# The FFN norm of a hybrid diffusion block: table load moved ahead, dg products of a tile queued together, the second tile's residual moved ahead

## The chip, the cores and the metric

One core of one Trainium2 chip. The metric is the device time of one execution in microseconds (us), as the median of several runs. PE is the matrix engine, ACT the scalar engine, DVE the vector engine, SP the queue that issues the loads.

## The reference

The kernel computes one layer of a parallel-branch backbone block for 256 tokens of width 2048, all in fp32. The change lies where the mixer's half ends and the feed-forward half (FFN) begins:

```
        x = x + g_m * yl
        x = x + g_f * _swiglu(_rmsnorm(x, norm_ffn_w[l]) * (1 + sc_f) + sh_f,
                              w_ffn_gate[l], w_ffn_up[l], w_ffn_down[l])
```

Here `yl = merged @ w_out` is the mixer's output, `_rmsnorm` divides each token's row by the root of its mean square, and `_swiglu(h)` is `(silu(h @ w_gate) * (h @ w_up)) @ w_down`, with `w_gate` and `w_up` of 2048x5632. The layer ends with a last RMSNorm.

## The kernel before

**Products in three terms.** Every large product is made in a rounded format, so each fp32 operand is split into a high part and a low part. `split` (L123 to L125) does it with a CAST on ACT (the high part, L124) and a subtraction on DVE (the low part, L125). `mm3` (L130 to L133) then issues three products: high by high (L131), activation high by weight low (L132), activation low by weight high (L133). One 128-row piece of the contraction for one half of the tokens is thus three products of 128x512.

**Stages.** The whole kernel is one list of stages. A stage is 256 rows of one weight matrix, 512 columns wide: it is loaded into one of 5 `raw` buffers, split into one of 3 `whi`/`wlo` pairs (or into a longer-lived `hhi`/`hlo` pair where `held=True`), and then multiplied. `stream` walks the list. Before the products of stage i it issues the loads up to stage i+5 and the splits up to stage i+2 (`LEAD` is 2), so the CAST and subtraction of a later stage's weights stand in the queues of ACT and DVE ahead of the work that stage i itself issues there. The order of instructions on each engine is the order in which this code is written, and each engine runs its own queue strictly in order. With 3 pairs, the CAST of one stage waits until PE is done with the stage three before it.

**Two token tiles.** The 256 tokens are two tiles of 128, tile 0 and tile 1, and the 2048 channels are four blocks of 512, numbered n. For the last block of `w_out` (`phase_o(3)`) the eight stages (p from 0 to 7, 256 rows each) are arranged so that tile 0 ends first: for p up to 4 both tiles are multiplied (`mm_both`), for the last three (`APART` is 3) first tile 0 alone (`mm_first`), and then tile 1 for these three together (`mm_second`). The first three stages of the gate matrix (`APART2` is 3) go the same way: `mm_gate0(p)` multiplies tile 0 for p = 0, 1, 2, then `mm_gate1` multiplies tile 1 for the three; `mm_gate(p)` from p = 3 on does both. Gate stages 0 and 1 need block 0 of the normalised activations, stages 2 and 3 block 1, stages 4 and 5 block 2.

**The norm of one tile**, with these names:
- `residual(n, t, ps)` (L1160 to L1165): DVE multiplies the accumulator `ps` by the gate `gm` and adds the input rows `xr`, giving `x`; ACT squares it and sums the row into `xss`.
- `rstd` (L1153 to L1158): DVE sums the four blocks' sums (`r`, L1155), ACT takes the root (L1156), DVE the reciprocal (L1157).
- `preload_sqrt` (L1149 to L1151): an ACT instruction on one column, ahead of which the compiler puts the load of the table set with the root.
- `dg` (L1173): DVE scales the identity matrix by `r`, so that a product of `x` with `dg` (L1182) both turns the tile so that channels lie on partitions and divides each row by its norm. A block has four such fp32 products, and the trace counts each as two passes of PE. They go into one of the four `aux` accumulators.
- `h`: the four pieces of a block are scaled by `Af` and shifted by `Sf`: on ACT for even blocks (L1188), on DVE for odd ones (L1186).
- `h2h`, `h2l`: the high and low part of `h` (L124 and L125), which the gate products take.

Of the kernel before, what the change touches and what calls it, by code (L numbers as in the profile page):

```python
# [11 lines left out]
F32 = mybir.dt.float32  # L12
F32R = mybir.dt.float32r
AF = mybir.ActivationFunctionType
ALU = mybir.AluOpType

P = 128
# [52 lines left out]
APART, APART2 = 3, 3  # L70
# [12 lines left out]
def hybrid_block(ctx: ExitStack, tc, io):  # L83
# [3 lines left out]
    V, S, T = nc.vector, nc.scalar, nc.tensor  # L87
# [12 lines left out]
    def nm(s):  # L100
        names[0] += 1
        return f"{s}{names[0]}"
# [4 lines left out]
    def H(shape, dt=F32, nme="h"):  # L107
        return hp.tile(shape, dt, tag="H", name=nm(nme))

    def Q(shape, dt=F32, nme="q"):  # L110
        return qp.tile(shape, dt, tag="Q", name=nm(nme))

    def acc(shape=(P, CH)):
        return psp.tile(list(shape), F32, tag="acc", name=nm("acc"))

    def aux(shape=(P, CH)):
        return psp.tile(list(shape), F32, tag="aux", name=nm("aux"))

    def C(shape, dt=F32, nme="c"):
        n = nm(nme)  # L120
        return cst.tile(shape, dt, tag=n, name=n)

    def split(hi, lo, src):  # L123
        S.copy(hi, src)  # L124
        V.tensor_tensor(lo, src, hi.bitcast(F32), ALU.subtract)  # L125
# [4 lines left out]
    def mm3(out, ah, al, bh, bl, first, last):  # L130
        T.matmul(out, ah, bh, start=first, stop=False)  # L131
        T.matmul(out, ah, bl, start=False, stop=False)  # L132
        T.matmul(out, al, bh, start=False, stop=last)  # L133
# [34 lines left out]
    def spawn(key, gen, front=False):  # L168
        beside.insert(0, (key, gen)) if front else beside.append((key, gen))
# [9 lines left out]
    def need(*keys):  # L179

        for key in keys:
            while key not in ended:
                credit[0] -= abs(step(next(e for e in beside if e[0] == key)))
# [32 lines left out]
    def add(src, n, mm, **kw):  # L216
        stages.append(Stage(src, n, mm, **kw))
        return stages[-1]
# [7 lines left out]
    ONE, ID = cc[:, CC_ONE : CC_ONE + P], cc[:, CC_ID : CC_ID + P]  # L226
# [210 lines left out]
    Af = C([P, KT], nme="Af")  # L437
    Sf = C([P, KT], nme="Sf")
# [4 lines left out]
    class Ada:  # L443
# [4 lines left out]
        def __init__(self, off, h, kt):  # L448
            self.off, self.h, self.kt = off, h, kt
            c0 = off + h * 1024  # L450
            self.src = w_ada[kt * P : (kt + 1) * P, c0 : c0 + 1024]
# [56 lines left out]
    def ada_keys(*offs):  # L508
        return [f"ada{off}{h}" for off in offs for h in range(2)]
# [328 lines left out]
    def mm_pair(ps, op, p, parts, ts, first, last):  # L838
        hi, lo = parts
        for t in ts:  # L840
            for k in range(2):
                ah, al = op(2 * p + k, t)
                mm3(ps[t], ah, al, hi[:, k, :], lo[:, k, :], first and k == 0, last and k == 1)
# [299 lines left out]
    x1 = [None] * 4  # L1143
    xss = C([P, 2, 4], nme="xss")
    h2h = [None] * 4
    h2l = [None] * 4
    xrs = {}

    def preload_sqrt(dep):  # L1149
        j = C([P, 1], nme="pre")  # L1150
        S.activation(j, dep, AF.Sqrt)  # L1151

    def rstd(ss, n):  # L1153
        r = C([P, n], nme="r")
        V.tensor_reduce(r, ss, mybir.AxisListType.X, ALU.add)  # L1155
        S.activation(r, r, AF.Sqrt, bias=eps, scale=1.0 / D)  # L1156
        V.reciprocal(r, r)  # L1157
        return r  # L1158

    def residual(n, t, ps):  # L1160
        xo = x1[n]
        V.tensor_tensor(xo[:, t, :], ps, gm[n][:, n % 2, :], ALU.mult)
        V.tensor_tensor(xo[:, t, :], xo[:, t, :], xrs[n][:, t, :], ALU.add)
        junk = Q([P, CH], nme="junk")
        S.activation(junk, xo[:, t, :], AF.Square, accum_out=xss[:, t, n : n + 1])  # L1165

    def norm_ffn(t):

        if t == 0:
            preload_sqrt(xss[:, 0, 0:1])  # L1170
        r = rstd(xss[:, t, :], 1)
        dg = Q([P, P], nme="dg")
        V.tensor_scalar(dg, ID, r, None, ALU.mult)  # L1173
        if t == 0:
            for n in range(4):
                h2h[n], h2l[n] = H([P, 4, 256], F32R, nme="h2h"), H([P, 4, 256], F32R, nme="h2l")

        def turn(n):
            ps = aux([P, 4, P])
            hf = Q([P, 4, P], nme="h2")  # L1180
            for c in range(4):
                T.matmul(ps[:, c, :], x1[n][:, t, c * P : (c + 1) * P], dg, start=True, stop=True)  # L1182
            for c in range(4):
                kt = 4 * n + c
                if n % 2:
                    V.tensor_scalar(hf[:, c, :], ps[:, c, :], Af[:, kt : kt + 1], Sf[:, kt : kt + 1], ALU.mult, ALU.add)  # L1186
                else:
                    S.activation(hf[:, c, :], ps[:, c, :], AF.Identity, bias=Sf[:, kt : kt + 1], scale=Af[:, kt : kt + 1])  # L1188
            o = slice(t * P, (t + 1) * P)
            split(h2h[n][:, :, o], h2l[n][:, :, o], hf)  # L1190

        return turn

    op_m, op_h2 = pair_op(mh, ml), pair_op(h2h, h2l)
    pg0 = []
# [1 line left out]
    def ask_x(n):  # L1197
        xrs[n] = H([P, 2, CH], nme="xr")
        load(xrs[n], x[:, n * CH : (n + 1) * CH].rearrange("(t p) n -> p t n", p=P))
        x1[n] = H([P, 2, CH], nme="x1")  # L1200

    def phase_o(n):
        def first():
            need("M0", "M1", "M2")
            ask_x(n)

        def run(ps):
            need(*ada_keys(G_M)[n // 2 : n // 2 + 1])
            for t in range(2):
                residual(n, t, ps[t])  # L1210
                yield 1.2

        if n < 3:
            tokens(io["w_out"], 0, KT, n * CH, op_m, lambda ps: spawn(f"o{n}", run(ps), True), first)
            if n == 0:
                stages[-2].first = lambda: need("M3")
            return

        ps = []
        turns = {}  # L1220
        n_o = 8 - APART
        held = []

        def mm_both(p):
            def mm(parts):
                if p == 0:
                    ps.extend((acc(), acc()))
                mm_pair(ps, op_m, p, parts, range(2), p == 0, False)
            return mm

        def mm_first(p):
            def mm(parts):
                held.append(parts)
                mm_pair(ps, op_m, p, parts, (0,), False, p == 7)
                if p == 7:
                    need("o0", "o1", "o2", *ada_keys(G_M, SC_F, SH_F))
                    residual(3, 0, ps[0])
                    turns[0] = norm_ffn(0)
            return mm

        def mm_second(parts):
            for p in range(n_o, 8):
                mm_pair(ps, op_m, p, held[p - n_o], (1,), False, p == 7)
            turns[0](0)
            residual(3, 1, ps[1])
            turns[1] = norm_ffn(1)
            for i in range(1, 4):
                turns[0](i)

        held2 = []  # L1250

        def mm_gate0(p):
            def mm(parts):
                if p == 0:
                    pg0.extend((acc(), acc()))
                held2.append(parts)
                mm_pair(pg0, op_h2, p, parts, (0,), p == 0, False)
                if p == APART2 - 1:
                    turns[1](0)
            return mm  # L1260

        def mm_gate1(parts):
            for p in range(APART2):
                if p + 1 < 4:
                    turns[1](p + 1)
                mm_pair(pg0, op_h2, p, held2[p], (1,), p == 0, False)
            for i in range(APART2 + 1, 4):
                turns[1](i)

        def mm_gate(p):  # L1270
            def mm(parts):
                mm_pair(pg0, op_h2, p, parts, range(2), False, p == 7)
            return mm

        for p in range(n_o):
            add(rows(io["w_out"], 2 * p, 2, 3 * CH, CH), CH, mm_both(p), first=(lambda: ask_x(3)) if p == 0 else None)
        for p in range(n_o, 8):
            add(rows(io["w_out"], 2 * p, 2, 3 * CH, CH), CH, mm_first(p), held=True, room=0)
            stages[-1].lead = p - n_o + 3
        add(None, 0, mm_second, room=0)  # L1280
        for p in range(APART2):
            add(rows(io["w_ffn_gate"], 2 * p, 2, 0, CH), CH, mm_gate0(p), room=0, held=p == 0)
        add(None, 0, mm_gate1, room=0)
        for p in range(APART2, 8):
            st = add(rows(io["w_ffn_gate"], 2 * p, 2, 0, CH), CH, mm_gate(p))
        st.after.append(lambda: (tanh_gate(0, pg0), spawn("a0", silu(0, pg0), True)))
# [292 lines left out]
```

## Time and profile before

| | |
|---|---|
| median of 3 runs | 1893.85 us (1893.33 to 1894.34) |
| the profiled execution, its own time | 1891.34 us |
| its span in the trace | 1889.5 us |
| PE busy | 1837.7 us, 97% of the span |
| DVE busy, ACT busy | 1249.3 us (66%), 851.5 us (45%) |
| mean granted clock of PE | 0.994 |

The span runs from the first to the last instruction that the profiler records; the execution's own time has 1.84 us around it. All stretches are read from the profiled execution, whose time is 2.51 us below the median of the three runs. A row of the timeline gives the start in us from the span's start, the duration, the engine, the line, the operation, out<-in, the count, and in brackets how long the engine was idle before it and who ended that. Products overlap on PE: one of 128x512 lasts 0.39 us and the next starts 0.227 us after it.

### The profile page before, as it was taken

The numbers are of one execution on the slowest core, as the hardware profiler recorded it, in microseconds if no ns is written. First come the engines' busy times: TensorE is split into PE (matmuls) and PEld (weight loads), VectorE is DVE, ScalarE is ACT, GpSimd is POOL, SyncE is SP. The second block draws the span as 40 slices with busy tenths as digits, with TensorE's granted clock in tenths as the row PEclk, the third lists the DMA queues.
The fourth block names the chain that finished last, engine by engine and source line by source line (L and its number), as shares of the span: only waits on it lengthen the run. The fifth ranks groups of instructions, "written<-read, shape, count | busy, mean of one in ns | idle before, by whom it ended". The sixth has DMA issues, their size and how long they took to land.

```text
span 1889.5 us, 23230 instructions
## 1 busy us (share of the span) xinstructions
PE 1837.7 (97%) x8796; PEld 1482.7 (78%) x8796; DVE 1249.3 (66%) x1524; ACT 851.5 (45%) x1200; POOL 0.2 (0%) x4
## 2 busy tenths in 40 slices
PE   5999999999999999999999998999999999999997
PEld 3667887777777777878788777888888888888886
DVE  4435784878787578887777755777655555555567
ACT  4323445647446464544444444444443444434444
POOL 0000000000000000000000000000000000000000
PEclk9999999999999999999999998999999999999999
DMA  9992342567667557888888854888756666656654
GB/s 325 355 349 76 112 123 67 168 183 228 196 211 224 150 162 232 292 267 304 284 292 292 294 182 134 281 267 303 262 189 191 195 184 190 193 195 189 191 190 143
DMA packets 211904, 409.19 MB, mean 217 GB/s; under 512 B 14672, under 2 KB 47568, under 8 KB 211792
## 3 DMA queue, kind: packets, MB, share of 16 engines
q1 hardware_dynamic: 211792, 407.71, 67.2%
q8 instruction: 69, 1.13, 0.2%
q14 instruction: 43, 0.35, 0.0%
HBM read 405.56 MB, written 2.10 MB: 216 GB/s over the span
## 4 chain that ended last, share of the span: by engine, by line
PE 90%; DVE 4%; ACT 3%; DMA 1%; issue 1%; SPq 1%; DVEq 0%; ACTq 0%
PE acc L131 26%; PE acc L132 26%; PE acc L133 26%; PE aux L314 2%; ACT whi L124 1%; PE aux L131 1%; DVE wlo L125 1%; PE aux L133 1%; PE aux L132 1%; PE aux L683 1%; PE aux L759 1%; SPq L105 1%; PE aux L1317 1%; PE aux L777 1%; DMA raw<-w_ada 0%
## 5 line engine op out<-in xcount | busy, mean ns | idle before, releaser
L125 DVE TENSOR_TENSOR wlo<-raw,whi 128x1024 fp32r<-128x1024 f32 x548 | 668.8, 1223 | 546.9 <-ACT whi L124 543.8
L124 ACT CAST whi<-raw 128x1024 fp32r<-128x1024 f32 x548 | 574.2, 1052 | 758.2 <-PE acc L133 650.6
L131 PE MATMUL acc<-whi,h2h 128*128 128x512 f32 x700 | 274.2, 392 | 5.9 <-ACT h2h L124 5.9
L133 PE MATMUL acc<-whi,h2l 128*128 128x512 f32 x700 | 273.2, 390 | 0.0
L132 PE MATMUL acc<-wlo,h2h 128*128 128x512 f32 x700 | 273.1, 390 | 0.0
L131 PE MATMUL acc<-whi,lh 128*128 128x512 f32 x640 | 256.6, 401 | 0.0
L132 PE MATMUL acc<-wlo,lh 128*128 128x512 f32 x640 | 249.6, 390 | 0.2 <-DVE wlo L125 0.2
L133 PE MATMUL acc<-whi,ll 128*128 128x512 f32 x640 | 249.6, 390 | 0.0
L131 PEld LDWEIGHTS acc<-whi,h2h 128*128 128x128 f32 x700 | 131.8, 188 | 33.6 <-ACT h2h L124 6.5
L133 PEld LDWEIGHTS acc<-whi,h2l 128*128 128x128 f32 x700 | 131.8, 188 | 28.4 <-DVE h2l L125 0.9
L461 DVE SCALAR_TENSOR_TENSOR adacc<-araw,sil,adacc 128x1024 f32<-128x1024 f32 x120 | 153.4, 1278 | 0.0
L132 PEld LDWEIGHTS acc<-wlo,h2h 128*128 128x128 f32 x700 | 131.9, 188 | 27.1
L132 PEld LDWEIGHTS acc<-wlo,lh 128*128 128x128 f32 x640 | 120.3, 188 | 26.9 <-issue 2.2
L131 PEld LDWEIGHTS acc<-whi,lh 128*128 128x128 f32 x640 | 120.2, 188 | 26.4 <-issue 1.5
L133 PEld LDWEIGHTS acc<-whi,ll 128*128 128x128 f32 x640 | 120.1, 188 | 25.5
L131 PE MATMUL acc<-whi,ah 128*128 128x512 f32 x336 | 131.0, 390 | 0.0
L133 PE MATMUL acc<-whi,al 128*128 128x512 f32 x336 | 130.7, 389 | 0.0
L132 PE MATMUL acc<-wlo,ah 128*128 128x512 f32 x336 | 130.7, 389 | 0.0
L131 PE MATMUL acc<-hh,whi 128*128 128x512 f32 x256 | 104.9, 410 | 3.6 <-ACT whi L124 3.6
L132 PE MATMUL acc<-hl,whi 128*128 128x512 f32 x256 | 100.7, 393 | 0.0
L133 PE MATMUL acc<-hh,wlo 128*128 128x512 f32 x256 | 100.5, 392 | 0.0
L133 PEld LDWEIGHTS acc<-whi,al 128*128 128x128 f32 x336 | 63.1, 188 | 13.1
(292 smaller groups left out, 2265.5 us busy)
## 6 DMA issues: line engine op xcount, KB each, us to landing
raw<-w_in SPq DMA_DIRECT2D x208, 512.0 KB, 4.2
araw<-w_ada SPq DMA_DIRECT2D x128, 512.0 KB, 4.9
raw<-w_ffn_gate SPq DMA_DIRECT2D x88, 512.0 KB, 4.5
raw<-w_ffn_up SPq DMA_DIRECT2D x88, 512.0 KB, 3.8
raw<-w_ffn_down SPq DMA_DIRECT2D x88, 512.0 KB, 3.6
raw<-w_ada SPq DMA_DIRECT2D x64, 512.0 KB, 9.4
raw<-w_ssd_out SPq DMA_DIRECT2D x32, 512.0 KB, 5.4
raw<-w_out SPq DMA_DIRECT2D x32, 512.0 KB, 5.0
```

Source lines behind the costliest of these rows:

```text
L105: nc.sync.dma_start(dst, src)
L124: S.copy(hi, src)
L125: V.tensor_tensor(lo, src, hi.bitcast(F32), ALU.subtract)
L131: T.matmul(out, ah, bh, start=first, stop=False)
L132: T.matmul(out, ah, bl, start=False, stop=False)
L133: T.matmul(out, al, bh, start=False, stop=last)
L314: T.matmul(aps[j][32 * k : 32 * k + 32, o], stat[:, 4 * p + k, :], raws[j, i][:, k, :], start=p == 0, stop=p == 3)
L461: V.scalar_tensor_tensor(a, self.raw, sil[:, kt : kt + 1], a, ALU.mult, ALU.add)
L683: T.matmul(ps, btk[:, 2 + t, :], xc[d][t], start=t == 0, stop=t == 1)
L759: T.matmul(seg, m, rh, start=n == 0, stop=n == 3)
L777: T.matmul(yps[b][(h % 2) * 64 : (h % 2) * 64 + 64, i // 2, t * P : (t + 1) * P], xl[:, t, h * HD : (h + 1) * HD], W[:, i, :], start=True, ...
L1317: T.transpose(ps[:, k, t * P : (t + 1) * P], a[t][:, c * P : (c + 1) * P], ID)
```

## The change

1. `preload_sqrt` is no longer called in the norm of tile 0 but in `mm_first` of the first of the three last stages of `w_out`. Its table load and its small instruction stand three stages earlier in ACT's queue.
2. `norm_ffn` and its closure `turn` are replaced by a class `Turn`, which issues the parts of a tile's norm singly: `norm` (root and `dg`), `mm(n)` (the four products of a block with `dg`), `mod(n)` (scale and shift to `h`), `cast(n)` (`h2h`), `low(n)` (`h2l`).
3. For tile 0, the products of all four blocks are written ahead of any `h`. The residual of tile 1 (its DVE part `residual_add`) follows the `h` of block 0, ahead of the `h` of block 1 and of every subtraction `h2l`; its squares follow the CAST of block 0.
4. The rest of tile 0 (blocks 2 and 3) is written behind the products of gate stage 0.
5. For tile 1, blocks 0 and 1 are written together, products, `h`, CAST and subtraction, behind gate stage 2 of tile 0; blocks 2 and 3 together behind gate stage 1 of tile 1. Before, block 0 stood there alone, and one block each stood ahead of a gate stage of tile 1.

The number of instructions of each kind is the same before and after.

```diff
-        if t == 0:
-            preload_sqrt(xss[:, 0, 0:1])
...
         def mm_first(p):
             def mm(parts):
+                if p == n_o:
+                    preload_sqrt(xss[:, 0, 0:1])
                 held.append(parts)
                 mm_pair(ps, op_m, p, parts, (0,), False, p == 7)
                 if p == 7:
                     need("o0", "o1", "o2", *ada_keys(G_M, SC_F, SH_F))
                     residual(3, 0, ps[0])
-                    turns[0] = norm_ffn(0)
+                    turn[0].norm()
...
         def mm_second(parts):
+            a, b = turn
             for p in range(n_o, 8):
                 mm_pair(ps, op_m, p, held[p - n_o], (1,), False, p == 7)
-            turns[0](0)
-            residual(3, 1, ps[1])
-            turns[1] = norm_ffn(1)
-            for i in range(1, 4):
-                turns[0](i)
+            for n in range(4):
+                a.mm(n)
+            a.mod(0)
+            residual_add(3, 1, ps[1])
+            a.mod(1)
+            a.cast(0)
+            residual_sq(3, 1)
+            a.low(0)
+            b.norm()
+            a.cast(1)
+            a.low(1)
...
                 mm_pair(pg0, op_h2, p, parts, (0,), p == 0, False)
+                if p == 0:
+                    for n in (2, 3):
+                        a.mod(n)
+                    for n in (2, 3):
+                        a.cast(n)
+                        a.low(n)
                 if p == APART2 - 1:
-                    turns[1](0)
+                    for n in range(2):
+                        b.mm(n)
+                        b.mod(n)
+                    for n in range(2):
+                        b.cast(n)
+                        b.low(n)
...
         def mm_gate1(parts):
+            b = turn[1]
             for p in range(APART2):
-                if p + 1 < 4:
-                    turns[1](p + 1)
                 mm_pair(pg0, op_h2, p, held2[p], (1,), p == 0, False)
-            for i in range(APART2 + 1, 4):
-                turns[1](i)
+                if p == 1:
+                    for n in (2, 3):
+                        b.mm(n)
+                        b.mod(n)
+                    for n in (2, 3):
+                        b.cast(n)
+                        b.low(n)
```

In the built programs the order shows as follows (out<-in; the numbers tell buffers apart and differ between the two programs). First ACT's queue at the end of `w_out`, before (-) against after (+); `hhi` and `whi` are the high parts of weights, `junk` the squares of `x`:

```order
 L124 CAST hhi_9152<-raw_9096 128x1024
-L124 CAST hhi_9164<-raw_9130 128x1024
-L124 CAST whi_9168<-raw_9148 128x1024
-L124 CAST whi_9182<-raw_9150 128x1024
-L1165 ACTIVATE junk_9194,xss_391<-x_9055 128x512
 L1151 ACT_TABLE_LOAD
-L1151 ACTIVATE pre_9196<-xss_391 128x1
+L1151 ACTIVATE pre_9156<-xss_391 128x1
+L124 CAST hhi_9166<-raw_9130 128x1024
+L124 CAST whi_9170<-raw_9148 128x1024
+L124 CAST whi_9184<-raw_9150 128x1024
+L1167 ACTIVATE junk_9196,xss_391<-x_9055 128x512
```

The table load has moved ahead of three CASTs of gate weights (stages 0, 1, 2) and ahead of the squares of tile 0's last block.

Next DVE's queue from tile 0's `dg` (the first row) on, before:

```order
L1173 TENSOR_SCALAR dg_9202<-cc_73,r_9198 128x128
L125 TENSOR_TENSOR h2l_9205<-h_9231,h2h_9204 128x4x128
L1162 TENSOR_TENSOR x_9055<-acc_9057,g_6359 128x512
L1163 TENSOR_TENSOR x_9055<-x_9055,xr_9053 128x512
L1155 TENSOR_REDUCE r_9246<-xss_391 128x1
L1157 RECIPROCAL r_9246<-r_9246 128x1
L1173 TENSOR_SCALAR dg_9250<-cc_73,r_9246 128x128
L1186 TENSOR_SCALAR h_9253<-aux_9252,Af_382,Sf_383 128x128 x4
L125 TENSOR_TENSOR h2l_9207<-h_9253,h2h_9206 128x4x128
```

and after:

```order
L1182 TENSOR_SCALAR dg_9202<-cc_73,r_9198 128x128
L1162 TENSOR_TENSOR x_9055<-acc_9057,g_6359 128x512
L1163 TENSOR_TENSOR x_9055<-x_9055,xr_9053 128x512
L1195 TENSOR_SCALAR h_9249<-aux_9227,Af_382,Sf_383 128x128 x4
L1207 TENSOR_TENSOR h2l_9255<-h_9242,h2h_9254 128x4x128
L1155 TENSOR_REDUCE r_9260<-xss_391 128x1
L1157 RECIPROCAL r_9260<-r_9260 128x1
L1182 TENSOR_SCALAR dg_9264<-cc_73,r_9260 128x128
L1207 TENSOR_TENSOR h2l_9267<-h_9249,h2h_9266 128x4x128
```

The residual of tile 1 (L1162, L1163) now stands ahead of the first `h2l`, and the `h` of block 1 (four instructions) ahead of the second tile's root and `dg` (from L1155 on), behind which it stood.

Last ACT's queue in the norm of tile 1, from the CAST of gate stage 3's weights (the first row) on, before:

```order
L124 CAST whi_9304<-raw_9162 128x1024
L1188 ACTIVATE h_9315<-aux_9314,Sf_383,Af_382 128x128 x4
L124 CAST h2h_9204<-h_9315 128x4x128
L124 CAST whi_9328<-raw_9178 128x1024
L124 CAST h2h_9206<-h_9333 128x4x128
L1188 ACTIVATE h_9351<-aux_9350,Sf_383,Af_382 128x128 x4
L124 CAST h2h_9208<-h_9351 128x4x128
L124 CAST h2h_9210<-h_9369 128x4x128
```

and after:

```order
L124 CAST whi_9304<-raw_9164 128x1024
L1197 ACTIVATE h_9319<-aux_9314,Sf_383,Af_382 128x128 x4
L1203 CAST h2h_9254<-h_9319 128x4x128
L1203 CAST h2h_9266<-h_9329 128x4x128
L124 CAST whi_9340<-raw_9180 128x1024
L1197 ACTIVATE h_9361<-aux_9356,Sf_383,Af_382 128x128 x4
L1203 CAST h2h_9288<-h_9361 128x4x128
L1203 CAST h2h_9292<-h_9371 128x4x128
```

The `h2h` of block 1 now stands ahead of the CAST of gate stage 4's weights (`whi_9328` before, `whi_9340` after), behind which it stood. On PE the order is the same but for one group: the four products with `dg` of tile 1's block 2 have moved from ahead of gate stage 1 of tile 1 to behind it.

More of the change, by code (lines that the diff above doesn't have):

```diff
@@ L1158, in rstd, with residual_add @@
         return r
-    def residual(n, t, ps):
+    def residual_add(n, t, ps):
         xo = x1[n]
@@ L1163, in residual, with residual_sq @@
         V.tensor_tensor(xo[:, t, :], xo[:, t, :], xrs[n][:, t, :], ALU.add)
+    def residual_sq(n, t):
         junk = Q([P, CH], nme="junk")
-        S.activation(junk, xo[:, t, :], AF.Square, accum_out=xss[:, t, n : n + 1])
-    def norm_ffn(t):
-        if t == 0:
-            preload_sqrt(xss[:, 0, 0:1])
[L1171 to L1180, printed above, removed]
+        S.activation(junk, x1[n][:, t, :], AF.Square, accum_out=xss[:, t, n : n + 1])
@@ L1181, in turn, with residual, __init__, norm @@
+    def residual(n, t, ps):
+        residual_add(n, t, ps)
+        residual_sq(n, t)
+    class Turn:
+        def __init__(self, t):
+            self.t, self.ps, self.hf = t, {}, {}
+        def norm(self):
+            r = rstd(xss[:, self.t, :], 1)
+            self.dg = Q([P, P], nme="dg")
+            V.tensor_scalar(self.dg, ID, r, None, ALU.mult)
+        def mm(self, n):
+            self.ps[n] = aux([P, 4, P])
             for c in range(4):
-                T.matmul(ps[:, c, :], x1[n][:, t, c * P : (c + 1) * P], dg, start=True, stop=True)
+                T.matmul(self.ps[n][:, c, :], x1[n][:, self.t, c * P : (c + 1) * P], self.dg, start=True, stop=True)
+        def mod(self, n):
+            self.hf[n] = Q([P, 4, P], nme="h2")
@@ L1183, in turn @@
             for c in range(4):
                 kt = 4 * n + c
+                a, b = Af[:, kt : kt + 1], Sf[:, kt : kt + 1]
                 if n % 2:
-                    V.tensor_scalar(hf[:, c, :], ps[:, c, :], Af[:, kt : kt + 1], Sf[:, kt : kt + 1], ALU.mult, ALU.add)
+                    V.tensor_scalar(self.hf[n][:, c, :], self.ps[n][:, c, :], a, b, ALU.mult, ALU.add)
                 else:
-                    S.activation(hf[:, c, :], ps[:, c, :], AF.Identity, bias=Sf[:, kt : kt + 1], scale=Af[:, kt : kt + 1])
@@ L1189, in turn, with cast, low @@
-            o = slice(t * P, (t + 1) * P)
-            split(h2h[n][:, :, o], h2l[n][:, :, o], hf)
-        return turn
+                    S.activation(self.hf[n][:, c, :], self.ps[n][:, c, :], AF.Identity, bias=b, scale=a)
+        def cast(self, n):
+            if h2h[n] is None:
+                h2h[n], h2l[n] = H([P, 4, 256], F32R, nme="h2h"), H([P, 4, 256], F32R, nme="h2l")
+            o = slice(self.t * P, (self.t + 1) * P)
+            S.copy(h2h[n][:, :, o], self.hf[n])
+        def low(self, n):
+            o = slice(self.t * P, (self.t + 1) * P)
+            V.tensor_tensor(h2l[n][:, :, o], self.hf[n], h2h[n][:, :, o].bitcast(F32), ALU.subtract)
@@ L1219, in phase_o @@
         ps = []
-        turns = {}
+        turn = (Turn(0), Turn(1))
         n_o = 8 - APART
@@ L1253, in mm @@
             def mm(parts):
+                a, b = turn
                 if p == 0:
```

## The prediction

> **What bounds the kernel now.** I read the first part of the page, then windows around the norm, then the timelines of PE, ACT and DVE there. The page says that PE is the bound:
>
> ```profile
> PE 1837.7 (97%) x8796; PEld 1482.7 (78%) x8796; DVE 1249.3 (66%) x1524; ACT 851.5 (45%) x1200; POOL 0.2 (0%) x4
> ```
>
> Windows of 3.4 us, which is how long the stretches at half clock in PE's rows last (columns: stretch, length, busy time and count of PE, PEld, DVE, ACT, POOL, granted clock, DMA share, GB/s):
>
> ```profile
> 1121.50:1124.90 3.40, 1.81 (x12) 1.30 (x11) 0.61 (x3) 2.03 (x5) 0.00 (x0) 1.00 0.57 219
> 1131.70:1135.10 3.40, 1.73 (x6) 1.16 (x7) 1.66 (x5) 2.37 (x6) 0.00 (x0) 1.00 0.00 0
> 1135.10:1138.50 3.40, 3.40 (x17) 3.30 (x15) 2.41 (x6) 1.36 (x3) 0.00 (x0) 0.51 0.00 0
> 1148.70:1152.10 3.40, 0.90 (x3) 0.48 (x4) 2.48 (x6) 1.57 (x5) 0.00 (x0) 1.00 0.51 141
> 1152.10:1155.50 3.40, 3.40 (x9) 2.66 (x10) 1.97 (x5) 1.33 (x4) 0.00 (x0) 0.52 0.06 18
> 1157.30:1400.00 242.70, 242.70 (x1092) 201.26 (x1091) 168.78 (x162) 104.87 (x112) 0.00 (x0) 1.00 0.79 262
> ```
>
> From 1157.30 on PE has no gap for 242 us. In the norm it has gaps, and after a window with 1.73 or 0.90 us of work in 3.40 the clock falls to half for the next 3.4 us (0.51, 0.52); after one with 1.81 it stays at 1.00. PE's timeline, the rows at each gap:
>
> ```profile
> 1122.25 0.39 PE L133 MATMUL acc<-hhi,ftl 128*128 128x512 f32 x1
> 1124.23 3.81 PE L1182 MATMUL aux<-dg,x 128*128 128x128 f32 x32 [1.59 <-DVE dg L1173]
> 1127.79 0.48 PE L131 MATMUL acc<-hhi,h2h 128*128 128x512 f32 x1
> 1128.34 0.49 PE L133 MATMUL acc<-hhi,h2l 128*128 128x512 f32 x1
> 1130.53 0.40 PE L133 MATMUL acc<-whi,h2l 128*128 128x512 f32 x1
> 1133.37 0.50 PE L131 MATMUL acc<-whi,h2h 128*128 128x512 f32 x1 [2.45 <-ACT h2h L124]
> 1135.13 3.58 PE L1182 MATMUL aux<-dg,x 128*128 128x128 f32 x16
> 1141.08 0.50 PE L131 MATMUL acc<-hhi,h2h 128*128 128x512 f32 x1 [2.37 <-ACT h2h L124]
> 1151.20 0.50 PE L131 MATMUL acc<-whi,h2h 128*128 128x512 f32 x1 [3.43 <-ACT h2h L124]
> 1157.28 0.39 PE L131 MATMUL acc<-whi,h2h 128*128 128x512 f32 x1
> ```
>
> The last row is the first product of gate stage 4. From 1122.48 (1122.25 and the 0.23 that a product takes before the next) to there it is 34.8 us. The work is 64 passes with `dg` at 0.111 (32 in 1124.23 to 1127.79) and 48 products at 0.227, together 18.0 us. So about 16.8 us are gaps and half clock; that is the most that any order can save here.
>
> **The first gap: the table load.** ACT's timeline:
>
> ```profile
> 1110.24 3.89 ACT L124 CAST hhi<-raw 128x1024 fp32r<-128x1024 f32 x4
> 1115.35 1.05 ACT L124 CAST whi<-raw 128x1024 fp32r<-128x1024 f32 x1 [1.22 <-DMA raw<-w_ffn_gate]
> 1117.47 1.05 ACT L124 CAST whi<-raw 128x1024 fp32r<-128x1024 f32 x1 [1.07 <-DMA raw<-w_ffn_gate]
> 1121.88 1.28 ACT L1151 ACT_TABLE_LOAD   x1
> 1125.39 1.50 ACT L1188 ACTIVATE h<-aux,Sf,Af 128x128 f32<-128x128 f32 x4 [1.83 <-PE aux L1182]
> 1126.93 0.62 ACT L124 CAST h2h<-h 128x512 fp32r<-128x512 f32 x1
> 1129.63 0.63 ACT L1165 ACTIVATE junk<-x 128x512 f32<-128x512 f32 x1 [2.08 <-DVE x L1163]
> 1130.58 0.29 ACT L1156 ACTIVATE r<-r,eps 128x1 f32<-128x1 f32 x1 [0.22 <-DVE r L1155]
> 1137.41 0.62 ACT L124 CAST h2h<-h 128x512 fp32r<-128x512 f32 x1 [2.04 <-DVE h L1186]
> 1146.91 1.04 ACT L124 CAST whi<-raw 128x1024 fp32r<-128x1024 f32 x1 [5.88 <-PE acc L133]
> 1150.53 0.62 ACT L124 CAST h2h<-h 128x512 fp32r<-128x512 f32 x1 [2.57 <-DVE h L1186]
> 1166.71 1.28 ACT L1296 ACT_TABLE_LOAD   x1
> ```
>
> and DVE's:
>
> ```profile
> 1118.55 1.23 DVE L125 TENSOR_TENSOR wlo<-raw,whi 128x1024 fp32r<-128x1024 f32 x1 [0.90 <-ACT whi L124]
> 1119.70 0.68 DVE L1162 TENSOR_TENSOR x<-acc,g 128x512 f32<-128x512 f32 x1
> 1121.89 0.16 DVE L1155 TENSOR_REDUCE r<-xss 128x1 f32<-128x4 f32 x1 [0.79 <-ACT junk L1165]
> 1123.79 0.29 DVE L1173 TENSOR_SCALAR dg<-cc,r 128x128 f32<-128x128 f32 x1
> 1127.58 0.69 DVE L125 TENSOR_TENSOR h2l<-h,h2h 128x512 fp32r<-128x512 f32 x1 [3.50 <-ACT h2h L124]
> 1128.90 0.69 DVE L1163 TENSOR_TENSOR x<-x,xr 128x512 f32<-128x512 f32 x1
> 1130.39 0.16 DVE L1155 TENSOR_REDUCE r<-xss 128x1 f32<-128x4 f32 x1 [0.79 <-ACT junk L1165]
> 1130.91 0.16 DVE L1157 RECIPROCAL r<-r 128x1 f32<-128x1 f32 x1 [0.36 <-ACT r L1156]
> 1131.11 0.28 DVE L1173 TENSOR_SCALAR dg<-cc,r 128x128 f32<-128x128 f32 x1
> 1131.31 1.36 DVE L1186 TENSOR_SCALAR h<-aux,Af,Sf 128x128 f32<-128x128 f32 x4
> ```
>
> In tile 0 `dg` starts 1.90 us after the row sum (1121.89 to 1123.79), in tile 1, where no load is in between, 0.72 (1130.39 to 1131.11). Without it `dg` starts at 1122.61 and PE, 0.44 later as before, at 1123.05: 1.18 earlier.
>
> What the load costs at its new place: the third CAST of the row at 1110.24 ends about 1113.2, so the load, and about 0.11 of its small instruction, push the fourth to 1114.6 and the next from 1115.35 to 1115.6; the one at 1117.47 waits for its transfer, so the delay ends there with 0.8 us to spare. The subtraction at 1118.55 and the residual behind it stay. Cost 0; the buffers freed some tenths later are loaded for stages that run 20 us later.
>
> [...] The row at 1166.71 stands right behind a CAST and takes 1.28, with no drain to be seen; I take that.
>
> **Tile 0, blocks 0 and 1.** PE's order does not change. Passes at 1123.05 to 1126.61; `h` of block 0 on ACT 1.16 behind PE's start (as 1124.23 to 1125.39), its CAST at 1125.75 to 1126.37. DVE does the residual of tile 1 meanwhile: 1.4 us from 1122.8, since PE ended tile 1's products at 1122.64. It is hidden under the wait of 3.50 that stood at 1127.58. Then `h` of block 1, when two blocks' passes are out: 1125.10 to 1126.46. Only then `h2l` of block 0, so the third gate product is at 1127.25, 0.6 behind the first instead of 0.55. From there to the 12th product's end as before (1128.34 to 1130.53, and 0.23): 1129.67.
>
> Tile 1's squares follow the CAST at 1126.3 (before 1129.63), the row sum at 1127.11, `dg` 0.72 later at 1127.83. The CAST of block 1 goes behind the root, at 1127.6 to 1128.2, its `h2l` to 1128.93. Both are ready before PE asks at 1129.67, so the gap of 2.45 is gone: gate stage 2 starts 3.70 earlier (1129.67 against 1133.37), and with no wait for its `h2l` its six products end at 1131.03, against 1135.13.
>
> **Tile 1.** `dg` has waited since 1128. Blocks 0 and 1 take 16 passes at full clock, 1.78, to 1132.81 (before 3.58 at half clock). ACT meanwhile ends blocks 2 and 3 of tile 0 (1.5 + 0.6 + 0.6, to 1130.9; CAST at 1137.41 before) and the CAST of gate stage 3 (to 1131.8), DVE likewise to 1133.1. So `h` of block 0 runs at 1132.19 to 1133.69, `h2h` at 1133.73 to 1134.35, the first product at 1134.40 and, behind `h` of block 1 and `h2l`, the third at 1135.21. This gap of 1.6 stays; it was 2.37 behind a half-clock stretch, with the product at 1141.08. So 6.68 earlier.
>
> The CAST at 1146.91 is where most of the rest goes. It waits 5.88 for PE, because its buffer is that of gate stage 1, whose tile 1 products come late; block 1's `h` and `h2h` (1150.53) stand behind it, and PE waits 3.43 for them. After, block 1 stands ahead of it: `h2h` ends at 1135.1, `h2l` at 1135.8. PE runs 12 products to 1137.48, 16 passes of blocks 2 and 3 to 1139.26, six products to 1140.62 and the 12 of gate stage 3 to 1143.34, where it was 1157.28.
>
> What is late next: blocks 2 and 3 of tile 1 now start only behind those 12 products. CAST of gate stage 4 at 1137.7, `h` at 1138.7, `h2h` at 1140.9, `h2l` of block 2 at about 1142.0; PE asks for it in tile 1 of gate stage 4 at 1143.34 + 1.36 = 1144.7. It is hidden with 2.7 us to spare. No DMA is moved; the loads of the next weights start earlier, when DVE frees their buffers.
>
> **The sum**: 1.18 (table) + 2.52 (second gap) + 0.40 (stage 2) + 2.58 (tile 1's first block) + 7.26 (the last gap, with its half clock) = 13.9 us off the span. The profiled execution would take 1891.34 - 13.9 = 1877.4; the median lies 2.51 above that execution, so the median should be about 1880.
>
> Unknown: the clock. A gap of 1.6 with the short wait at the third product leaves 1.7 to 1.9 us of work if it falls into one window, between the rows of 1.73 and 1.81 that decided differently; half clock for 3.4 us costs 1.7. I take none, since the windows may also split the gap, and keep 0 to 3.4 (two windows) for the range. The three half-clock windows of before may be two or four in another execution: 1.7 to either side.
>
> [...]
>
> **Rivals.**
> - Tile 1's first block stays the wait it was. If `h2h` came 5.95 behind the start of the passes, as before (1135.13 to 1141.08), the first product would be at 1136.98, 2.6 later than I have it, and a half-clock window would follow: 13.9 - 2.6 - 1.7 = 9.6, so 1884. For it: ACT is the chain there in both. Against: what held ACT (CAST at 1137.41, then the one behind it) is done by 1131.8.
> - The gain is given back downstream: DMA runs at a share of 0.79 in 1157.30 to 1400, and a PE that comes 14 us earlier could catch the loads. Against: loads are paced by buffers that PE itself frees, so all moves together, and PE has no gap there. If all is given back, 1894, no change.
> - Slower: blocks 2 and 3 of tile 1 come too late for gate stage 4. They have 2.7 us; past that each us is lost, and the kernel becomes slower only when they come 2.7 + 13.9 = 16.6 us later, by over 0.2% at 20.4. Their chain of a CAST, four `h`, two more CASTs and a subtraction is 5 us long, so only an order that lets them wait for a whole further stage could do it. At 21 us late the time would be 1898.
>
> **Chances.** My forecast 0.82, the first rival 0.09, given back 0.06, slower 0.03. The predicted time is 1880. The range goes down by 1.7 (one more half-clock window before) and some for step errors to 1877, and up past the first rival and its own window to 1886. Two runs of this kernel differ by about 0.05%; I call within 0.2% (1890.1 to 1897.6) no change. Faster 0.91, same 0.06, slower 0.03.
>
> **What would show it.** Right: no ACT_TABLE_LOAD between the squares and the root of tile 0; first `dg` pass some 0.4 us behind the last product; no gap at gate stage 2 of tile 0; one gap of 1 to 2 us at gate stage 0 of tile 1, and none behind it; about 20.9 us from 1122.5 to the first product of gate stage 4. Wrong: a CAST of weights that still stands waiting for PE ahead of an `h2h` that PE wants, a gap ahead of gate stage 4, or half-clock windows after the 1.6 us gap.

## The result, and the profile after

| | before | after |
|---|---|---|
| median | 1893.59 us (6 runs, 1892.11 to 1894.88) | 1879.74 us (6 runs, 1877.50 to 1880.89) |
| span of the profiled execution | 1889.5 us | 1876.9 us |
| last w_out product to gate stage 4, on PE | 34.80 us | 20.62 us |

The ratio is 0.9926 (95% interval 0.9915 to 0.9937): 0.74% faster. The third row, which the experiments below call the stretch, runs from 0.23 us behind the start of the last product of `w_out` to the start of gate stage 4's first product.

The first part of the page, after. The work of PE is nearly the same (1834.0 us where it was 1837.7); its share of the span went from 97% to 98%:

```profile
PE 1834.0 (98%) x8796; PEld 1480.8 (79%) x8796; DVE 1250.0 (67%) x1524; ACT 851.2 (45%) x1200; POOL 0.2 (0%) x4
```

PE's timeline after, the rows that answer to those shown of before (the norm starts 1.57 us later in this execution, so compare distances, not starts):

```profile
1123.82 0.39 PE L133 MATMUL acc<-hhi,ftl 128*128 128x512 f32 x1
1124.48 3.81 PE L1187 MATMUL aux<-dg,x 128*128 128x128 f32 x32 [0.28 <-DVE dg L1182]
1128.05 0.48 PE L131 MATMUL acc<-hhi,h2h 128*128 128x512 f32 x1
1128.60 0.49 PE L133 MATMUL acc<-hhi,h2l 128*128 128x512 f32 x1
1131.02 0.39 PE L131 MATMUL acc<-whi,h2h 128*128 128x512 f32 x1
1132.38 1.95 PE L1187 MATMUL aux<-dg,x 128*128 128x128 f32 x16
1135.68 0.50 PE L131 MATMUL acc<-hhi,h2h 128*128 128x512 f32 x1 [1.35 <-ACT h2h L1203]
1140.49 0.48 PE L131 MATMUL acc<-whi,h2h 128*128 128x512 f32 x1
1144.67 0.39 PE L131 MATMUL acc<-whi,h2h 128*128 128x512 f32 x1
```

Of the four gaps (1.59, 2.45, 2.37, 3.43) two are left, 0.28 ahead of tile 0's `dg` products and 1.35 ahead of tile 1's first product. Gate stage 2 starts without a wait in tile 0 (1131.02) and in tile 1 (1140.49), and the 16 passes take 1.95 us where they took 3.58 at half clock.

ACT after:

```profile
1111.85 2.94 ACT L124 CAST hhi<-raw 128x1024 fp32r<-128x1024 f32 x3
1114.81 1.28 ACT L1151 ACT_TABLE_LOAD   x1
1116.21 1.03 ACT L124 CAST hhi<-raw 128x1024 fp32r<-128x1024 f32 x1
1118.91 1.05 ACT L124 CAST whi<-raw 128x1024 fp32r<-128x1024 f32 x1 [0.71 <-DMA raw<-w_ffn_gate]
1127.71 0.63 ACT L1167 ACTIVATE junk<-x 128x512 f32<-128x512 f32 x1
1128.86 0.61 ACT L1203 CAST h2h<-h 128x512 fp32r<-128x512 f32 x1
1133.47 1.50 ACT L1197 ACTIVATE h<-aux,Sf,Af 128x128 f32<-128x128 f32 x4 [0.40 <-PE aux L1187]
1135.01 1.38 ACT L1203 CAST h2h<-h 128x512 fp32r<-128x512 f32 x2
1138.99 1.04 ACT L124 CAST whi<-raw 128x1024 fp32r<-128x1024 f32 x1 [2.60 <-PE acc L133]
```

The table load stands between two CASTs and takes 1.28 us, and its delay ends at 1118.91, where the CAST of gate stage 2's weights waits for its transfer. Tile 1's two `h2h` run back to back at 1135.01, and the CAST that waits for PE (1138.99, formerly 5.88, now 2.60) stands behind them.

DVE after:

```profile
1124.05 0.29 DVE L1182 TENSOR_SCALAR dg<-cc,r 128x128 f32<-128x128 f32 x1
1124.25 0.68 DVE L1162 TENSOR_TENSOR x<-acc,g 128x512 f32<-128x512 f32 x1
1126.55 1.37 DVE L1195 TENSOR_SCALAR h<-aux,Af,Sf 128x128 f32<-128x128 f32 x4 [0.88 <-PE aux L1187]
1127.84 0.69 DVE L1207 TENSOR_TENSOR h2l<-h,h2h 128x512 fp32r<-128x512 f32 x1
1129.19 0.29 DVE L1182 TENSOR_SCALAR dg<-cc,r 128x128 f32<-128x128 f32 x1
1142.48 1.46 DVE L1207 TENSOR_TENSOR h2l<-h,h2h 128x512 fp32r<-128x512 f32 x2
```

The residual of tile 1 starts 0.2 us behind the start of tile 0's `dg` (1124.05) and runs while PE and ACT make block 0, and tile 1's `dg` is done at 1129.48, 2.9 us before PE asks for it (1132.38).

Windows after (same columns as before):

```profile
1131.70:1135.10 3.40, 2.63 (x20) 2.31 (x18) 3.11 (x6) 2.97 (x7) 0.00 (x0) 1.00 0.01 2
1135.10:1138.50 3.40, 2.82 (x11) 2.08 (x12) 1.94 (x4) 1.14 (x2) 0.00 (x0) 1.00 0.57 154
1157.30:1400.00 242.70, 242.70 (x1091) 201.38 (x1091) 168.44 (x162) 102.69 (x110) 0.00 (x0) 1.00 0.80 262
```

No stretch of the norm runs at half clock any more. Behind it PE is full as before, and from gate stage 4 to the end of the span it takes 732.2 us in both executions (1889.5 - 1157.28 and 1876.9 - 1144.67): nothing is given back.

### The profile page after: what moved, and what is told of

The parts are those of the page before. It is cut to its first block, busy times and chain, and to the rows that moved or that the text cites. A ratio compares the mean times of both kernels' runs of the same rounds, so it can differ in the third digit from the quotient of the medians.

```text
span 1876.9 us, 23230 instructions
## 1 busy us (share of the span) xinstructions
PE 1834.0 (98%) x8796; PEld 1480.8 (79%) x8796; DVE 1250.0 (67%) x1524; ACT 851.2 (45%) x1200; POOL 0.2 (0%) x4
## 4 chain that ended last, share of the span: by engine, by line
PE 90%; DVE 4%; ACT 3%; DMA 2%; issue 1%; SPq 1%; DVEq 0%; ACTq 0%
PE acc L131 26%; PE acc L132 26%; PE acc L133 26%; PE aux L314 2%; ACT whi L124 1%; DVE wlo L125 1%; PE aux L131 1%; PE aux L132 1%; PE aux L133 1%; PE aux L683 1%; PE aux L759 1%; DVE adacc L461 1%; SPq L105 1%; PE aux L1357 1%; PE aux L777 1%
## 5 line engine op out<-in xcount | busy, mean ns | idle before, releaser
L132 PEld LDWEIGHTS acc<-wlo,ah 128*128 128x128 f32 x336 | 63.1, 188 | 13.1
```

## The experiments

The theory: the 14 us are three orders in a chain. The table load is a step of about 1.2 us in front; tile 0's order lets tile 1's root and ACT's last blocks come early; tile 1's order takes block 1 out from behind a CAST that waits for PE. The three half-clock stretches of before (3.4 us each) come with the gaps of 2.45, 2.37 and 3.43 us and go with them. The rival: one of them alone carries the gain.

| kernel | last w_out product | gate stage 4 | stretch | median, runs | ratio to before |
|---|---|---|---|---|---|
| table load alone | 1124.39 | 1158.68 | 34.29 | 1892.82, 11 | 0.9996 [0.9987, 1.0005] |
| after, table load back | 1123.99 | 1145.73 | 21.74 | 1879.80, 5 | 0.9927 [0.9914, 0.9939] |
| after, tile 0 old | 1124.61 | 1153.10 | 28.49 | 1885.96, 5 | 0.9960 [0.9946, 0.9973] |
| after, tile 1 old | 1124.41 | 1150.87 | 26.46 | 1884.24, 5 | 0.9954 [0.9941, 0.9966] |
| before, no wait of the CAST | 1126.93 | 1156.81 | 29.88 | 1889.04, 9 | 0.9973 [0.9964, 0.9983] |
| after, tile 1 one stage earlier | 1122.64 | 1141.98 | 19.34 | 1877.40, 5 | 0.9919 [0.9904, 0.9933] |
| after, once more | 1125.25 | 1146.15 | 20.90 | 1880.22, 5 | 0.9926 [0.9914, 0.9939] |
| after, block 2's dg products ahead | 1122.50 | 1143.40 | 20.90 | 1877.44, 1 | |

(The second column is the start of the last product plus 0.23.)

### The table load alone

```diff
-        if t == 0:
-            preload_sqrt(xss[:, 0, 0:1])
         r = rstd(xss[:, t, :], 1)
...
             def mm(parts):
+                if p == n_o:
+                    preload_sqrt(xss[:, 0, 0:1])
                 held.append(parts)
```

> The kernel before with one part of the change: the table load for the root stands three stages earlier, all else is as before. The stretch of PE from its last w_out product to the first product of gate stage 4 was 34.8 us before and is 20.6 after the whole change. My theory: the gap ahead of tile 0's dg products shrinks from 1.6 to about 0.3 us and everything behind it comes 1.2 us earlier; stretch 33.6, time about 1892.4. Rival one (the chain behind is set by something else, so the part alone does nothing): stretch 34.8, 1893.6. [...]

PE's timeline of this run:

```profile
1125.10 3.81 PE L1180 MATMUL aux<-dg,x 128*128 128x128 f32 x32 [0.55 <-DVE dg L1171]
1136.03 1.95 PE L1180 MATMUL aux<-dg,x 128*128 128x128 f32 x16
1141.97 0.79 PE L131 MATMUL acc<-hhi,h2h 128*128 128x512 f32 x1 [3.99 <-ACT h2h L124]
```

The first gap is down by 1.04, and tile 1's first product comes 17.58 us behind the last product of `w_out` instead of 18.60, so the whole chain did move by 1.0. But the stretch is only 0.5 shorter, not the 1.2 of my theory. Before, one stretch of half clock fell on the 16 passes (3.58), which lay hidden beside ACT's chain. Here they ran at full clock (1.95) and the gap behind them grew to 3.99. The products behind the gap then had 5.0 us of half clock (granted clock 0.50 from 1141.97 to 1146.95), where the same products had 3.4 us of it before (0.70 over 5.63 us, from 1141.08 to 1146.71). The time cannot tell this from no change, so neither my 1892.4 nor rival one's 1893.6 is decided by it; the trace decides against that rival. At its new place the load took 1.28 us, between two CASTs.

### The table load put back

```diff
-                if p == n_o:
-                    preload_sqrt(xss[:, 0, 0:1])
                 held.append(parts)
...
+                    preload_sqrt(xss[:, 0, 0:1])
                     turn[0].norm()
```

> The changed kernel with the table load back in its old place, between the squares and the root of tile 0. My theory: the first gap is 1.6 us again and all else stays, so the stretch is 20.6 + 1.2 = 21.8 us and the time about 1881. Rival (the table load is what the change lives from, since an early dg lets all later work start early): most of the 14 us comes back, stretch over 28, time over 1887.

PE's timeline:

```profile
1125.58 3.81 PE L1187 MATMUL aux<-dg,x 128*128 128x128 f32 x32 [1.43 <-DVE dg L1182]
1136.74 0.50 PE L131 MATMUL acc<-hhi,h2h 128*128 128x512 f32 x1 [1.35 <-ACT h2h L1203]
```

The first gap is 1.43 and the next again 1.35: everything is the changed kernel, 1.12 us later, and the stretch of 21.74 is the forecast one. The rival falls. In the time, 1879.80, the load's place is not to be seen.

### Tile 0 in the old order

```diff
-            for n in range(4):
-                a.mm(n)
-            a.mod(0)
-            residual_add(3, 1, ps[1])
-            a.mod(1)
-            a.cast(0)
-            residual_sq(3, 1)
-            a.low(0)
-            b.norm()
-            a.cast(1)
-            a.low(1)
+            a.mm(0)
+            a.mod(0)
+            a.cast(0)
+            a.low(0)
+            residual(3, 1, ps[1])
+            b.norm()
+            for n in range(1, 4):
+                a.mm(n)
+                a.mod(n)
+                a.cast(n)
+                a.low(n)
...
-                if p == 0:
-                    for n in (2, 3):
-                        a.mod(n)
-                    for n in (2, 3):
-                        a.cast(n)
-                        a.low(n)
```

> The changed kernel with tile 0 in the old order (block 0 whole, then the residual and the root of tile 1, then blocks 1 to 3 one after the other); table load and tile 1 as after. My theory: the gap of 2.45 us ahead of gate stage 2 of tile 0 returns, blocks 2 and 3 of tile 0 end later on ACT, and tile 1's first product comes about 5.5 us later than after; no gap ahead of gate stage 2 of tile 1. Stretch 26 to 28 us, time 1885 to 1887. Rival (the order of tile 0 is worth only its own gap): stretch 23, time about 1882.3.

PE's timeline:

```profile
1134.41 0.50 PE L131 MATMUL acc<-whi,h2h 128*128 128x512 f32 x1 [2.48 <-ACT h2h L1203]
1142.12 0.50 PE L131 MATMUL acc<-hhi,h2h 128*128 128x512 f32 x1 [4.01 <-ACT h2h L1203]
```

On ACT, the last `h2h` of tile 0 (block 3) and the first `h` of tile 1:

```profile
1138.45 0.62 ACT L1203 CAST h2h<-h 128x512 fp32r<-128x512 f32 x1 [2.04 <-DVE h L1195]
1139.92 1.50 ACT L1197 ACTIVATE h<-aux,Sf,Af 128x128 f32<-128x128 f32 x4
```

The gap of 2.45 is back as 2.48, and the first product of tile 1 waits 4.01, at 17.5 us into the stretch instead of 11.6. The stretch is 7.87 us longer than the changed kernel's, and 0.5 above my 26 to 28; 1.7 of the 7.87 is a half-clock stretch behind the 4.01. So this order is worth far more than its own gap: PE's gap is 2.5, but ACT's lateness with blocks 2 and 3 is carried into tile 1, whose first `h` starts 15.3 us into the stretch instead of 9.4 (1133.47 after). The rival (stretch 23) falls. The run undoes the whole order of tile 0 at once: what the residual's place, block 1's `h` ahead of the second root, or the place of blocks 2 and 3 is worth alone is not shown.

### Tile 1 in the old order

```diff
                 if p == APART2 - 1:
-                    for n in range(2):
-                        b.mm(n)
-                        b.mod(n)
-                    for n in range(2):
-                        b.cast(n)
-                        b.low(n)
+                    b.mm(0)
+                    b.mod(0)
+                    b.cast(0)
+                    b.low(0)
...
+                b.mm(p + 1)
+                b.mod(p + 1)
+                b.cast(p + 1)
+                b.low(p + 1)
                 mm_pair(pg0, op_h2, p, held2[p], (1,), p == 0, False)
-                if p == 1:
-                    for n in (2, 3):
...
```

> The changed kernel with tile 1 in the old order (block 0 behind gate stage 2 of tile 0, one further block ahead of each gate stage of tile 1); table load and tile 0 as after. My theory: the CAST of gate stage 4's weights stands ahead of block 1 again and waits for PE, so PE waits about 3.5 us ahead of gate stage 2 of tile 1 and may lose 1.7 more at half clock; stretch 24 to 27 us, time 1883 to 1886. Rival (with tile 0 early, block 1 is in time whatever stands ahead of it): stretch 21, time 1880.

The CAST of gate stage 4's weights on ACT, the `h2h` of block 1 behind it, and the product on PE that waits for it:

```profile
1140.48 1.04 ACT L124 CAST whi<-raw 128x1024 fp32r<-128x1024 f32 x1 [4.29 <-PE acc L133]
1144.09 0.62 ACT L1203 CAST h2h<-h 128x512 fp32r<-128x512 f32 x1 [2.57 <-DVE h L1195]
```

```profile
1144.76 0.50 PE L131 MATMUL acc<-whi,h2h 128*128 128x512 f32 x1 [3.43 <-ACT h2h L1203]
```

The gap of 3.43 stands there to the hundredth as before the change, though tile 0 is early: a circle. The CAST waits for PE's gate stage 1 of tile 1, block 1 stands behind the CAST, and PE's gate stage 2 waits for block 1, so the gap was as long wherever it fell: 3.43 before, with the table load alone, and here. The stretch is 5.84 longer than after, 1.7 of it half clock behind the gap.

### The wait alone taken away

In the kernel before, gate stage 1 keeps its weights in a pair of its own, so the pair that the CAST writes is free:

```diff
-            add(rows(io["w_ffn_gate"], 2 * p, 2, 0, CH), CH, mm_gate0(p), room=0, held=p == 0)
+            add(rows(io["w_ffn_gate"], 2 * p, 2, 0, CH), CH, mm_gate0(p), room=0, held=p < 2)
```

> The kernel before with one edit: gate stage 1's weights are kept in a longer-lived pair, so that the CAST of gate stage 4's weights reuses a pair that has long been free. The order of all instructions stays; only the wait of that CAST for PE (5.88 us before) is taken away. My theory: block 1 of tile 1 is then ready when PE asks, the gap of 3.43 us ahead of gate stage 2 of tile 1 and the half clock behind it go; stretch from the last w_out product to gate stage 4 about 29.5 us instead of 34.8, time about 1888.5. Rival (ACT and DVE simply have too much to do there, the wait is only where their lateness shows): stretch 34 to 35, time 1893.

The same CAST on ACT, and on PE the passes of tile 0 and the last gap in the norm:

```profile
1146.55 1.04 ACT L124 CAST whi<-raw 128x1024 fp32r<-128x1024 f32 x1
```

```profile
1129.04 5.44 PE L1182 MATMUL aux<-dg,x 128*128 128x128 f32 x32 [1.96 <-DVE dg L1173]
1146.70 0.80 PE L131 MATMUL acc<-hhi,h2h 128*128 128x512 f32 x1 [4.01 <-ACT h2h L124]
```

With no order changed, the CAST waits for nothing, and the gap of 3.43 is gone. The rival falls. The stretch is 4.9 us shorter than before, but that is not the price of the wait: from tile 1's first product to gate stage 4 it is 6.1 shorter (10.11 us against 16.20), while the part ahead of it is 1.2 longer (19.77 against 18.60). There the first gap was 1.96 instead of 1.59, and half clock fell on the 32 passes (5.44 us instead of 3.81). So it is partly luck that 29.88 lies so near my 29.5. That the 5.88 and the 3.43 are one wait, and not general lateness of ACT and DVE, is shown.

### One step more

```diff
-                if p == APART2 - 1:
+                if p == APART2 - 2:
                     for n in range(2):
                         b.mm(n)
```

> The changed kernel with one step more: blocks 0 and 1 of tile 1 are written behind gate stage 1 of tile 0 instead of behind gate stage 2, so their 16 passes run ahead of the six products of that stage and their h on ACT stands ahead of the CAST of gate stage 3's weights. My theory: the last gap of 1.35 us (PE waits for tile 1's first h2h) is filled by those six products; stretch 19.2 us instead of 20.6, no gap above 0.5 us, time about 1.4 lower than the changed kernel, 1878.3. Rival (ACT is the chain, and the CAST of gate stage 3, now behind, comes too late for PE): stretch 20.6 or more, with a gap ahead of gate stage 3.

ACT's two rows, tile 1's first `h` and the CAST of gate stage 3 now behind it, and the only row of PE in the norm with a gap:

```profile
1130.76 1.51 ACT L1197 ACTIVATE h<-aux,Sf,Af 128x128 f32<-128x128 f32 x4
1133.59 1.04 ACT L124 CAST whi<-raw 128x1024 fp32r<-128x1024 f32 x1
```

```profile
1123.15 3.81 PE L1187 MATMUL aux<-dg,x 128*128 128x128 f32 x32 [0.35 <-DVE dg L1182]
```

The stretch is 19.34, 1.3 above the 18.0 of pure work, and the gap of 1.35 is filled. The rival's gap ahead of gate stage 3 is not there. The median is 2.8 below the changed kernel's on the same chip, but their intervals against before overlap widely (0.9904 to 0.9933, 0.9914 to 0.9939): the trace shows the gain in the norm, the time does not separate the two.

### The yardstick, and the dg products queued together

> The changed kernel once more, on the chip of the other three runs, as the yardstick for them. My theory: stretch 20.6 us, time 1879 to 1881; where it differs from the first time, the difference is in whole stretches of 3.4 us at half clock (1.7 us each), mostly outside the norm. Rival: the norm itself varies, stretch 19 to 23.

The changed kernel once more: the stretch differs by 0.28, all in the first gap (0.56 instead of 0.28). The CAST of gate stage 2's weights, which waits for its transfer, and tile 0's `dg` in this run:

```profile
1120.39 1.05 ACT L124 CAST whi<-raw 128x1024 fp32r<-128x1024 f32 x1 [1.01 <-DMA raw<-w_ffn_gate]
1125.54 0.29 DVE L1182 TENSOR_SCALAR dg<-cc,r 128x128 f32<-128x128 f32 x1
```

From the CAST to `dg` it is 5.15 us here and 5.14 in the first trace (1118.91 to 1124.05), since tile 0's residual stands on DVE behind the subtraction of these weights. But the CAST starts 4.86 us ahead of the end of `w_out` here and 5.14 there, so the 0.28 comes from when a transfer ended, measured against PE. Outside the norm the two spans differ by 1.2 us, not by a whole 1.7 as I had it.

The other has the `dg` products of tile 1's block 2 back ahead of gate stage 1:

```diff
+                if p == 1:
+                    b.mm(2)
                 mm_pair(pg0, op_h2, p, held2[p], (1,), p == 0, False)
                 if p == 1:
                     for n in (2, 3):
-                        b.mm(n)
+                        if n == 3:
+                            b.mm(n)
                         b.mod(n)
```

> The changed kernel with the dg products of tile 1's block 2 ahead of gate stage 1 of tile 1, where they stood before, so that this tile's products are not queued together in twos; the order on ACT and DVE stays. My theory: nothing waits for them there and PE does the same work, so the stretch stays at 20.6 us within 0.2, which would show that queueing the products together is worth nothing by itself. Rival: the products' place matters, since the CAST of gate stage 4 waits for PE to end gate stage 1, now 0.9 us later; stretch 21.5.

Its stretch, in the only execution of this kernel, is 20.90, with a first gap of 0.51 and the second again at 1.35:

```profile
1134.34 0.50 PE L131 MATMUL acc<-hhi,h2h 128*128 128x512 f32 x1 [1.35 <-ACT h2h L1203]
```

That is 0.3 above the 20.6 of my theory, but equal to the yardstick's 20.90: the products' place is worth nothing that one trace could show. In tile 0 there was nothing to try: on PE all four blocks' products stood together before the change too.

## Why the prediction was right

Forecast 1880.0 (1877 to 1886), measured 1879.74; 13.85 off the median, 14.2 off the stretch, where the sum had 13.9. That the time agrees to 0.3 us is partly luck, for the six runs after span 3.4 us; the distances on PE are the better test.

Distances from the end of the last `w_out` product, forecast and found:

| step | forecast | after |
|---|---|---|
| first dg pass of tile 0 | 0.57 | 0.43 |
| gate stage 2 of tile 0 | 7.19 | 6.97 |
| 16 passes of tile 1 | 8.55 | 8.33 |
| tile 1's first product | 11.92 | 11.63 |
| gate stage 4 | 20.86 | 20.62 |

- **Table load.** The forecast of no cost at the new place held: the CAST of gate stage 2's weights waited 0.71 us for its transfer all the same. From that CAST to tile 0's `dg` it is 6.32 us with the load in between (1117.47 to 1123.79) and 5.14 without it, which is the term of 1.18; putting the load back cost 1.12 on PE. Alone, in the kernel before, it would have been worth 0.5 and not 1.18: the first gap was shorter there, but the half clock fell elsewhere (5.0 us of it on the products behind tile 1's gap instead of 3.4), and more than half of the term was taken back.
- **Tile 0.** The residual of tile 1 was hidden under the wait for `h2h`, as forecast, and `h2l` of block 0, written behind block 1's `h`, was still ready in time: from 1128.05 to the third product it is 0.55 us as before. I had 0.64. The terms of 2.52, 0.40 and 2.58, together 5.50, are what the sum had for tile 1's first product beside the load; with tile 0's order undone it came 5.88 later (17.51 against 11.63).
- **Tile 1.** The gap that I kept is there. From the first of the 16 passes to the first product it is 3.30 us (1132.38 to 1135.68), where I had 3.37. The profile calls it 1.35 and not 1.6, since it counts from the end of the last pass (1.95 behind the first) and I from where the next could start (1.78).
- **The last gap.** My term of 7.26 for it holds the CAST's wait, its half clock and the half clock ahead of it. From tile 1's first product to gate stage 4 it is 16.20 us before and 8.99 after, 7.21 less. Undoing tile 1's order gives 5.84 back, and taking the wait alone away in the kernel before saves 6.1 here. The single undoings add up to 1.12 + 7.87 + 5.84 = 14.8 against the first trace (the whole is 14.2) and to 0.84 + 7.59 + 5.56 = 14.0 against the yardstick's 20.90 (the whole is 13.9): within the 0.28 by which the two differ, taken three times, the parts add up to the whole.
- **Blocks 2 and 3 of tile 1.** The last `h2l` of the two is done at 1143.94, and PE asks for block 2 in tile 1 at 1144.67 + 1.36 = 1146.03, so they have over 2 us to spare. The forecast of 2.7 was for block 2 alone, whose `h2l` is the first of the two.
- **Clock.** I left open whether a gap of 1.6 would bring half clock, with 1.7 to 1.9 us of work in a window. In all five traces with a gap of 1.35 there it did not, and after, 3.40 us around the gap held 2.05 us of work (last section), so it was less close than I had it. The line that I drew between 1.73 and 1.81 is not firm either: in the kernel with the CAST's wait taken away, 1.67 us of work in 3.41 was followed by full clock (last section). What sets the limit stays open, and that it goes by the work in a window was my estimate from the rows of 1.73, 0.90 and 1.81.
- **The profiled executions** differ by 12.6 and not 13.9, because after started the norm 1.57 later. One stretch of half clock ahead of the norm, shown below, accounts for that (1.7).

## What to carry to other kernels

When an engine works through its queue in order, look for the instruction that waits for the engine it feeds: here a CAST into a buffer that PE still read stood ahead of the CAST that PE wanted next, and moving one ahead of the other ended PE's wait (the CAST still waited 2.60 us, with nothing behind it that PE wanted yet), while giving it a free buffer ended both. Write the steps that the bound engine will ask for first ahead of prefetches that cannot run yet, and spread a short chain's parts so that its latency lies under other work of the bound engine. A gap of PE can cost more than its length: before, half clock for 3.4 us, which costs 1.7, followed each of the gaps of 2.45, 2.37 and 3.43 us. So a part can be worth less alone than within the whole (here 0.5 against 1.1 us for the table load); undo each part of the change to learn what it is worth, and look where the half clock fell before the difference is put down to the part.

## What the runs showed of the hardware

The same code with the same gaps ran at full clock in one execution and at half clock in another. Windows over a place far ahead of the norm, 672 to 682, before and then after:

```profile
672.00:682.00 10.00, 7.90 (x30) 5.63 (x31) 9.59 (x15) 1.71 (x3) 0.00 (x0) 1.00 0.37 105
```

```profile
672.00:682.00 10.00, 8.35 (x26) 5.56 (x27) 8.12 (x13) 1.07 (x2) 0.00 (x0) 0.83 0.36 105
```

Both have gaps of 1.61 and 0.64 us there. Of the ten traces of this study four show the half clock at this place (after, the table load alone, tile 1 old, no wait of the CAST) and six do not, each time for about 3.4 us, which costs 1.7. Without their stretch of the norm the ten spans differ by 4.5 us (1854.7 to 1859.2) with nearly the same code; when the half clock between the first 60 us and the norm is taken off, as windows of 3.4 us over each span show it (none to two such stretches, 1.7 each), they lie within 1.2. Much of what separates two runs of this kernel is thus how many of its gaps were followed by half clock.

The window of 3.40 us around the gap of 1.35 after, and, in the kernel with the CAST's wait taken away, a window of 3.41 us with a gap of 1.74 and the one behind it (the half clock on the 32 passes had ended at 1132.61 there):

```profile
1132.60:1136.00 3.40, 2.05 (x17) 1.83 (x16) 3.11 (x7) 2.83 (x7) 0.00 (x0) 1.00 0.21 19
```

```profile
1136.03:1139.44 3.41, 1.67 (x8) 0.96 (x6) 2.33 (x8) 1.43 (x4) 0.00 (x0) 1.00 0.00 0
1139.44:1142.85 3.41, 3.25 (x22) 2.61 (x20) 2.04 (x6) 1.52 (x4) 0.00 (x0) 1.00 0.00 0
```

The work of PE in a window, as this column counts it, did not decide alone in these traces: 1.67 was followed by full clock here, 1.73 by half clock before.

Half clock also followed short gaps: those of 1.61 and 0.64 us after, at the place shown above, and one of 1.96 us ahead of the 32 passes in the kernel with the CAST's wait taken away.
